# The opening loads of a two-layer encoder trunk, put into one fixed order on SyncE's queue

## The chip, the cores and the metric

The kernel runs on one core of a Trainium2 chip (trn2). Its time is the device time of one execution in microseconds (us). The engines are TensorE (PE, with its weight loads as PEld), VectorE (DVE), ScalarE (ACT), GpSimd (POOL) and SyncE (SP, which here only issues DMAs). The trace was taken by the hardware profiler in one execution; its times count from the start of that execution's span.

## The reference, cut to what matters

The trunk has two layers over x of 512 tokens by 1024 channels, all in float32, and a memory of 256 tokens by 1024. Only the start of the first layer matters here:

```python
for l in range(DEPTH):                       # DEPTH = 2
    h = rms_norm(x, norm_g[l])               # a sum of squares over 1024 channels per token
    proj = h @ w_in[l]                       # 7752 columns: three branches, gates, indexer
    ...
    mkv = rms_norm(mem, mem_norm_g[l]) @ w_mem_kv[l]
    mk, mv = jnp.split(mkv, 2, axis=-1)      # memory keys and values, 512 columns each
    y_mem = memory_attention(mq, mk, mv) * jax.nn.silu(mz)
    ...
    x = x + merged @ w_out[l]
return rms_norm(x, final_g)
```

## The kernel before

Every float32 product is made of three matmuls on parts in the type float32r: a value is split into hi (a cast on ACT) and lo (value minus hi, on DVE or POOL), and hi times hi, hi times lo and lo times hi are added up in PSUM. So each weight tile of 128x1024 (512 KB) that comes in through the tile `wraw` costs one cast to `whi` and one subtraction to `wlo`; each of these three names has four buffers.

The opening of the first layer needs four sets of loads, 7168 KB in all: `mem`, the memory (4 loads of 256 KB, line 257 in `load_mem`); the keys' weights `w_mk0` (512 KB for each of four steps, the first as two halves, lines 326 and 328); `x` (8 loads of 256 KB, line 339); and the values' weights `w_mv` (4 of 512 KB, line 166 in `raw_chunk`, called at line 345). All are issued by SyncE on one DMA queue. Each `w_mv` load takes a `wraw` buffer that a `w_mk0` tile held, so it has to wait until that tile's last subtraction (line 335) is done.

What is done with them, in PE's order, which the source fixes with `issue_after` (through `behind_pe`) from line 357 on:

- Lines 349 to 356: the key products, 96 matmuls of 256 columns, over `mem` and `w_mk0`. They are not scaled by the memory's norm yet; that is done later.
- Line 358, `norm_cols(sums)`: the sums of squares of x over its channels, 8 matmuls against a column of ones (each shows as two in the trace, on the tile `tr`). Before them ACT squares each x tile (line 228) and DVE adds the squares of tiles 1 to 6 to those of tile 0 (line 231); those of tile 7 go to PE by themselves. After them DVE (line 214) and POOL (line 215, a power) make the column 1/rms.
- Lines 368 to 370, `mem_v` of chunk 0: 12 matmuls of 512 columns. It needs chunk 0 of `w_mv` split (lines 346 and 347: casts behind the last square on ACT, subtractions on DVE).
- Line 372, `spread`: the norm of x is spread to a bank of PSUM, which `norm_x` (line 381, on DVE and ACT) needs to make h.
- `mem_v` of chunk 1; then the sums of squares of the memory (lines 376 to 380), which ACT squares (line 365) and POOL adds (line 367, behind the power of line 215); `mem_v` of chunk 2; `spread` of the memory's norm; `mem_v` of chunk 3.
- Line 437: the first projection of h, for the indexer; from there on PE works through the rest of the layer.

The framework's scheduler sets the order of the instructions on each engine, out of what is ready, by priorities from its own model. `issue_after(a)` adds an edge: the instructions traced in the block that run on the engine of `a` come behind `a` on it. It sets an order of issue, and no wait for `a` to end. Before the change no such edge bears on the loads: the `issue_after` at line 344 names an ACT instruction, and the load in its block is issued by SyncE.

Of the kernel before, what the change touches and what calls it, by code (L numbers as in the profile page):

```python
# [1 line left out]

# [1 line left out]

# [14 lines left out]
P = 128  # L19
# [4 lines left out]
KT = D // P  # L24
# [28 lines left out]
def kernel(  # L53
# [18 lines left out]
    nc = tc.nc  # L72
# [10 lines left out]
    on_pe, on_pool, on_act, on_dve, on_sp = [], [], [], [], []  # L83
# [8 lines left out]
    def nm(base):  # L92
        count[0] += 1
        return f"{base}_{count[0]}"
# [7 lines left out]
    def s2(base, dt=F32, shape=(P, S)):  # L102
        return work.tile(list(shape), dt, tag="s2", name=nm(base), bufs=N_S2)
# [60 lines left out]
    def raw_chunk(src, n=1024):  # L164
        raw = wpool.tile([P, 1024], F32, tag="wraw", name=nm("wraw"), bufs=4)
        nc.sync.dma_start(raw[:, :n], src)
        return raw
# [57 lines left out]
    def norm_add(sums, k, xk, n=S, apart=KT - 1):  # L225

        sq = s2("sq")[:, :n]
        on_act[:] = [A.activation(sq, xk, AF.Square)]
        last = on_act[0]
        if k not in (0, apart):  # L230
            last = V.tensor_add(sums[0], sums[0], sq)  # L231
        else:
            sums.append(sq)
        return last
# [18 lines left out]
    def load_mem(ks=range(0, KT, 2)):  # L253
        ms = []
        for k in ks:
            t = s2("mem", shape=(P, 2, M))
            on_sp[:] = [nc.sync.dma_start(t, memT[k * P:(k + 2) * P, :].rearrange("(a p) m -> p a m", p=P))]
            ms.append(t)
        return ms

    def mem_parts(l, m, k):
        hi = s2("memh", F32R, (P, 2, M))
        lo = s2("meml", F32R, (P, 2, M))
        for a in range(2):
            g = 20 * l + G_MEM + k + a
            on_dve[:] = [split_scaled(hi[:, a, :], lo[:, a, :], m[:, a, :], gains[:, g:g + 1])]
        return [hi[:, 0, :], hi[:, 1, :]], [lo[:, 0, :], lo[:, 1, :]]
# [50 lines left out]
    mem0, mh, ml, parts_k = [], [], [], []  # L318
    for i in range(4):
        raw, hi, lo = (wpool.tile([P, 1024], t, tag=g, name=nm(g), bufs=4)  # L320
                       for t, g in ((F32, "wraw"), (F32R, "whi"), (F32R, "wlo")))
        mem0 += load_mem((2 * i,))
        for a in range(2):
            if i == 0:
                c = slice(a * 512, (a + 1) * 512)
                nc.sync.dma_start(raw[:, c], w_mk0[i, :, c])
            elif a == 0:
                nc.sync.dma_start(raw, w_mk0[i])
        a, b = mem_parts(0, mem0[i], 2 * i)
        mh += a  # L330
        ml += b
        for a in range(2):
            c = slice(a * 512, (a + 1) * 512)
            A.copy(hi[:, c], raw[:, c])
            last = V.tensor_sub(lo[:, c], raw[:, c], hi[:, c])
        parts_k.append((hi, lo))
    x = [s2("x") for _ in range(KT)]
    for k in range(KT):
        nc.sync.dma_start(x[k], xT[k * P:(k + 1) * P, :])
    sums, parts_v = [], []  # L340
    for k in range(KT):
        last = norm_add(sums, k, x[k])
        if k in (1, 3, 5, 6):
            with tc.issue_after(on_act[0].ins):
                parts_v.append(raw_chunk(w_mv[0, len(parts_v)]))
    with tc.issue_after(on_act[0].ins), tc.issue_after(last.ins):
        parts_v[:2] = [split_chunk(raw, eng=V) for raw in parts_v[:2]]
    banks, pv = [pj(), pj()], [pj(), bank("pv")]
    for k in range(KT):
        hi, lo = parts_k[k // 2]  # L350
        for h in range(4):
            o = banks[h // 2][:, h % 2 * M:h % 2 * M + M]
            c = slice(k % 2 * 512 + h * P, k % 2 * 512 + h * P + P)
# [80 lines left out]
    for l in range(DEPTH):  # L434
# [420 lines left out]
        x = []  # L855
# [136 lines left out]
```

## Time and profile before

| | |
|---|---|
| median of 3 runs | 1077.87 us (1077.76 to 1078.63) |
| the profiled execution | 1077.09 us, of which the span of the trace is 1075.3 us |
| PE busy | 1054.9 us, 98% of the span |
| PE without work in the opening | 6.3 us, before the sums of squares of x |
| DMA in the opening | 7168 KB by about 23 us, close to 390 GB/s from 4 to 20 us |

The profiled execution's 1.8 us outside the span are what lies ahead of the first and behind the last instruction of the trace. In views of a stretch the busy time of PE is that of matmuls, which overlap each other; PEclk is the granted clock of TensorE, where 1.00 is 2.4 GHz and 0.50 is 1.2 GHz. On the rows of a timeline the text in brackets is the engine's idle time before that row, and what ended it. Rows that are marked SPq are the issues of DMAs by SyncE, not the transfers.

### The profile page before, as it was taken

Reading aid. Unit: us, or ns where it says so; the run is one execution under the profiler, and the core shown is the slowest. Engines: PE = TensorE matmul, PEld = TensorE weight load, DVE = VectorE, ACT = ScalarE, POOL = GpSimd, SP = SyncE. Lnnn points to the kernel's source line nnn. Section 1 sums busy time; section 2 is a strip of 40 time slices with the busy share of each in tenths; the row PEclk is TensorE's granted clock in tenths of the full one; section 3 lists DMA queues with packets and bytes.
Section 4 is the critical chain, followed back from the end, with each engine's and each line's share of the span. In section 5 each row is a group of like instructions: output and inputs, shape, how many; then the busy total and the mean of one; then the engine's idle time right before and its main releaser. Section 6 shows DMA issues by size and latency. Waiting matters only on the chain.

```text
span 1075.3 us, 13884 instructions
## 1 busy us (share of the span) xinstructions
PE 1054.9 (98%) x5108; PEld 889.5 (83%) x5108; DVE 704.1 (65%) x1305; ACT 477.3 (44%) x858; POOL 215.0 (20%) x296
## 2 busy tenths in 40 slices
PE   7999999999999999999999999999999999999997
PEld 6888888888788887888888888888888888788886
DVE  5857968787678855534465688787858887444343
ACT  6645454322465543433345555532235654333332
POOL 1400420000324411121250133100005323002101
PEclk8999999999999999999999999999999999999998
DMA  7454212323322222425444222121333222133312
GB/s 278 129 169 145 88 60 79 98 79 118 108 89 98 98 65 80 134 94 196 147 125 151 79 89 79 59 98 60 118 112 115 89 98 79 59 98 98 128 69 79
DMA packets 38804, 113.82 MB, mean 106 GB/s; under 512 B 4264, under 2 KB 8360, under 8 KB 38736
## 3 DMA queue, kind: packets, MB, share of 16 engines
q1 hardware_dynamic: 37440, 110.81, 31.0%
q10 hardware_dynamic: 1296, 2.12, 0.5%
q8 instruction: 40, 0.66, 0.2%
q14 instruction: 28, 0.23, 0.1%
HBM read 108.70 MB, written 6.84 MB: 107 GB/s over the span
## 4 chain that ended last, share of the span: by engine, by line
PE 92%; DVE 3%; ACT 1%; DMA 1%; issue 1%; POOL 1%; SPq 0%; POOLq 0%; DVEq 0%; ACTq 0%
PE pj L86 75%; PE at L86 7%; PE pv L86 5%; PE tr L547 2%; PE tr L86 2%; DVE wlo L151 1%; POOL sg L689 1%; DMA wraw<-in_w_mk 1%; DVE sq L231 1%; ACT whi L172 1%; DMA x<-in_xT 1%; DVE p L745 0%; DVE sg L685 0%; DVE stk L462 0%; ACT mgh L158 0%
## 5 line engine op out<-in xcount | busy, mean ns | idle before, releaser
L172 ACT CAST whi<-wraw 128x1024 fp32r<-128x1024 f32 (+1 forms) x174 | 181.7, 1046 | 369.7 <-PE pj L86 237.7
L86 PE MATMUL pj<-hh,whi 128*128 128x512 f32 (+1 forms) x848 | 330.1, 389 | 0.0
L86 PE MATMUL pj<-hl,whi 128*128 128x512 f32 (+1 forms) x848 | 328.8, 388 | 0.0
L86 PE MATMUL pj<-hh,wlo 128*128 128x512 f32 (+1 forms) x848 | 328.5, 387 | 0.0
L151 DVE TENSOR_TENSOR wlo<-wraw,whi 128x1024 fp32r<-128x1024 f32 x156 | 194.5, 1250 | 136.9 <-ACT whi L172 136.3
L86 PEld LDWEIGHTS pj<-hh,wlo 128*128 128x128 f32 x848 | 159.2, 188 | 32.1
L86 PEld LDWEIGHTS pj<-hh,whi 128*128 128x128 f32 x848 | 159.3, 188 | 31.0
L86 PEld LDWEIGHTS pj<-hl,whi 128*128 128x128 f32 x848 | 159.3, 188 | 30.7
L689 POOL TENSOR_TENSOR sg<-sg,sg 128x512 f32<-128x512 f32 x32 | 48.5, 1515 | 230.9 <-DVE sg L685 230.9
L86 PE MATMUL pj<-yh,whi 128*128 128x512 f32 x192 | 75.1, 391 | 0.0
L86 PE MATMUL pj<-yl,whi 128*128 128x512 f32 x192 | 74.8, 390 | 0.0
L86 PE MATMUL pj<-yh,wlo 128*128 128x512 f32 x192 | 74.8, 389 | 0.0
L731 POOL TENSOR_TENSOR p<-rel,acc 128x256 f32<-128x256 f32 (+2 forms) x48 | 60.1, 1276 | 0.0
L685 DVE SCALAR_TENSOR_TENSOR sg<-sg,pj 128x512 f32<-128x512 f32 x48 | 32.8, 685 | 36.7 <-PE pj L86 36.6
L86 PE MATMUL pj<-mgl,whi 128*128 128x512 f32 (+1 forms) x152 | 54.3, 357 | 0.3 <-DVE mgl L159 0.3
L86 PE MATMUL pj<-mgh,whi 128*128 128x512 f32 (+1 forms) x152 | 54.2, 357 | 0.0
L86 PE MATMUL pj<-mgh,wlo 128*128 128x512 f32 (+1 forms) x152 | 54.1, 356 | 0.0
L529 DVE MATCH_REPLACE8 acc<-m,acc 128x256 f32<-128x256 f32 (+2 forms) x96 | 51.4, 542 | 0.0
L745 DVE CUSTOM_DVE_ANT_0 p<-at,p 128x128 f32<-128x128 f32 (+1 forms) x64 | 29.4, 489 | 32.6 <-PE at L86 32.4
L528 DVE MAX8 m<-acc 128x8 f32<-128x256 f32 (+2 forms) x96 | 48.7, 547 | 0.0
L86 PEld LDWEIGHTS pj<-yh,wlo 128*128 128x128 f32 x192 | 36.0, 188 | 7.5
L86 PEld LDWEIGHTS pj<-yl,whi 128*128 128x128 f32 x192 | 36.1, 188 | 7.3
(211 smaller groups left out, 1683.3 us busy)
## 6 DMA issues: line engine op xcount, KB each, us to landing
wraw<-in_w_tiled SPq DMA_DIRECT2D x112, 512.0 KB, 3.4
wraw<-in_w_br SPq DMA_DIRECT2D x24, 512.0 KB, 3.5
wraw<-in_w_out SPq DMA_DIRECT2D x16, 512.0 KB, 3.4
wraw<-in_w_mv SPq DMA_DIRECT2D x8, 512.0 KB, 3.5
x<-in_xT SPq DMA_DIRECT2D x16, 256.0 KB, 5.4
wraw<-in_w_av SPq DMA_DIRECT2D x8, 512.0 KB, 3.9
rel<-bias_row SPq DMA_DIRECT2D x16, 256.0 KB, 3.9
wraw<-in_w_mk SPq DMA_DIRECT2D x7, 512.0 KB, 3.6
```

Source lines behind the costliest of these rows:

```text
L86: on_pe[:] = [T.matmul(*a, **kw)]
L151: eng.tensor_sub(out_lo, src, hi)
L172: A.copy(hi[:, :n], raw[:, :n])
L231: last = V.tensor_add(sums[0], sums[0], sq)
L528: V.max(m8, a[:, :n])
L529: V.match_replace(out=a[:, :n], in_to_replace=m8, in_values=a[:, :n], imm_value=TAKEN)
L547: T.transpose(pt[:, i * P:(i + 1) * P], col_of(qb, kb), ident)
L685: last = V.scalar_tensor_tensor(s, s, 1.0, ps, op0=ALU.add, op1=ALU.mult)
L689: G.tensor_add(acc[j], acc[j], s)
L731: G.tensor_add(p[:, Q_COL[qb]:Q_COL[qb] + n], rel[:, 512 - n:512], mb[:, :n])
L745: V.tensor_tensor_reduce(out=pq, in0=ps[:, :n], in1=pq, op0=ALU.add, op1=ALU.min, scale=-1.0, scalar=3e38, accum_out=st[:, 0, qb:qb + 1])
```

## The change

Each load of the opening is put behind the one before it by `issue_after` on SyncE: memory and keys' weights in turn, as they are written, then x tiles 0 to 5; behind x tile 5 both the first chunk of `w_mv` and x tile 6, which have no order between them; then x tile 7; and the `w_mv` chunks 1 to 3 behind x tile 7 (none of them is put behind chunk 0 or behind each other). The list `on_sp` holds the load that was issued last; `load_mem` already set it. No load, tile or buffer is added or taken away, and nothing changes in what ACT, DVE, POOL and PE compute.

```diff
+        with tc.issue_after(on_sp[0].ins) if on_sp else nullcontext():
+            mem0 += load_mem((2 * i,))
-        mem0 += load_mem((2 * i,))
         for a in range(2):
             if i == 0:
                 c = slice(a * 512, (a + 1) * 512)
-                nc.sync.dma_start(raw[:, c], w_mk0[i, :, c])
+                with tc.issue_after(on_sp[0].ins):
+                    on_sp[:] = [nc.sync.dma_start(raw[:, c], w_mk0[i, :, c])]
             elif a == 0:
-                nc.sync.dma_start(raw, w_mk0[i])
+                with tc.issue_after(on_sp[0].ins):
+                    on_sp[:] = [nc.sync.dma_start(raw, w_mk0[i])]
...
     x = [s2("x") for _ in range(KT)]
-    for k in range(KT):
-        nc.sync.dma_start(x[k], xT[k * P:(k + 1) * P, :])
     sums, parts_v = [], []
     for k in range(KT):
+        with tc.issue_after(on_sp[0].ins):
+            on_sp[:] = [nc.sync.dma_start(x[k], xT[k * P:(k + 1) * P, :])]
+        if k == 5:
+            with tc.issue_after(on_sp[0].ins):
+                parts_v.append(raw_chunk(w_mv[0, 0]))
+    with tc.issue_after(on_sp[0].ins):
+        parts_v += [raw_chunk(w_mv[0, c]) for c in range(1, 4)]
+    for k in range(KT):
         last = norm_add(sums, k, x[k])
-        if k in (1, 3, 5, 6):
-            with tc.issue_after(on_act[0].ins):
-                parts_v.append(raw_chunk(w_mv[0, len(parts_v)]))
     with tc.issue_after(on_act[0].ins), tc.issue_after(last.ins):
         parts_v[:2] = [split_chunk(raw, eng=V) for raw in parts_v[:2]]
```

## Rows read from the trace of the kernel before

**Rows 1.** The head of the profile's page: the span, the busy time of each engine with its share of the span and its instructions, and PE's busy tenths in 40 equal slices of the span.
```profile
span 1075.3 us, 13884 instructions
...
PE 1054.9 (98%) x5108; PEld 889.5 (83%) x5108; DVE 704.1 (65%) x1305; ACT 477.3 (44%) x858; POOL 215.0 (20%) x296
...
PE   7999999999999999999999999999999999999997
```

**Rows 2.** The waits of PE over the whole span: what it waited for, us in total, how often, the longest.
```profile
PE tr L86 <- DVE sq L231: 7.3, 2, 6.3
```

**Rows 3.** The chain of work that ended last, in order of time, where it passes through the opening: start, us, what.
```profile
19.47 0.64 ACT sq L228
...
24.11 0.70 DVE sq L231
...
24.95 3.55 PE tr L86 x16
```

**Rows 4.** SyncE's issues, in order of time: start, us from the first start to the last end, line, what is loaded, how many in the row.
```profile
3.18 0.97 SPq L328 DMA_DIRECT2D wraw<-in_w_mk  x2
4.19 0.44 SPq L257 DMA_DIRECT2D mem<-in_memT  x1
6.74 2.64 SPq L166 DMA_DIRECT2D wraw<-in_w_mv  x2
9.43 0.43 SPq L257 DMA_DIRECT2D mem<-in_memT  x1
11.05 1.64 SPq L166 DMA_DIRECT2D wraw<-in_w_mv  x2
12.75 5.25 SPq L339 DMA_DIRECT2D x<-in_xT  x8
```

**Rows 5.** The waits of SyncE's queue up to 19 us: line, what it waited for, us in total, how often, the longest.
```profile
SPq L166 <- DVE wlo L335: 5.2, 4, 1.9
SPq L403 <- DMA x<-in_xT: 0.8, 1, 0.8
```

**Rows 6.** DMA issues by size with the us from issue to landing, each for the one issue in a stretch: the first `w_mv` load (issued at 6.74) and the third (11.05).
```profile
wraw<-in_w_mv SPq DMA_DIRECT2D x1, 512.0 KB, 5.6
wraw<-in_w_mv SPq DMA_DIRECT2D x1, 512.0 KB, 4.9
```

**Rows 7.** ACT in order of time, from 9 to 30 us: start, us, line, operation, out<-in, how many.
```profile
10.39 1.15 ACT L334 CAST whi<-wraw 128x512 fp32r<-128x512 f32 x2 [0.18 <-DMA wraw<-in_w_mk]
...
14.73 0.91 ACT L158 ACTIVATE memh<-mem,gains 128x256 fp32r<-128x256 f32 x2 [2.39 <-DMA mem<-in_memT]
18.80 3.34 ACT L228 ACTIVATE sq<-x 128x512 f32<-128x512 f32 x5 [3.15 <-DMA x<-in_xT]
22.33 1.94 ACT L228 ACTIVATE sq<-x 128x512 f32<-128x512 f32 x3 [0.20 <-DMA x<-in_xT]
24.18 3.87 ACT L172 CAST whi<-wraw 128x1024 fp32r<-128x1024 f32 x4
27.95 2.19 ACT L365 ACTIVATE sq<-mem 128x512 f32<-128x512 f32 x4
```

**Rows 8.** DVE in order of time, from 20 to 31 us.
```profile
20.14 4.67 DVE L231 TENSOR_TENSOR sq<-sq,sq 128x512 f32<-128x512 f32 x6 [3.98 <-ACT sq L228]
25.24 2.36 DVE L176 TENSOR_TENSOR wlo<-wraw,whi 128x1024 fp32r<-128x1024 f32 x2 [0.43 <-ACT whi L172]
28.54 0.16 DVE L214 TENSOR_SCALAR rs_v<-tr 128x4 f32<-128x4 f32 x1 [0.94 <-PE tr L86]
```

**Rows 9.** POOL in order of time, from 28 to 35 us.
```profile
28.79 1.94 POOL L215 TENSOR_TENSOR rs_r<-rs_v,mhalf 128x4 f32<-128x4 f32 x1 [25.11 <-DVE rs_v L214]
30.70 4.15 POOL L367 TENSOR_TENSOR sq<-sq,sq 128x512 f32<-128x512 f32 x3
```

**Rows 10.** PE in order of time, single rows: the sums of squares of x, the first matmul of `mem_v` chunk 0 and the eighth, the sums of squares of the memory and the matmul behind them, and the first matmul of the indexer's projection.
```profile
24.95 3.55 PE L86 MATMUL tr<-ones,sq 128*128 128x1 f32 x16 [6.25 <-DVE sq L231]
28.36 0.77 PE L86 MATMUL pj<-whi,memh 128*128 128x512 f32 x1
...
31.49 0.42 PE L86 MATMUL pv<-wlo,memh 128*128 128x512 f32 x1
...
36.33 0.95 PE L86 MATMUL tr<-ones,sq 128*128 128x1 f32 x8
37.14 0.49 PE L86 MATMUL pj<-whi,memh 128*128 128x512 f32 x1
...
43.20 0.40 PE L86 MATMUL tr<-hh,whi 128*72 128x512 f32 x1
```

**Rows 11.** Stretches of the opening: us, then busy time of PE, PEld, DVE, ACT and POOL with their instructions, the granted clock, the DMA engines' share, GB/s.
```profile
20.00:22.00 2.00, 0.00 (x0) 0.00 (x0) 1.66 (x3) 1.85 (x4) 0.00 (x0) 0.82 0.93 322
...
30.00:32.00 2.00, 2.00 (x7) 1.51 (x7) 0.98 (x1) 0.14 (x1) 2.00 (x2) 0.62 0.87 244
```

**Rows 12.** The same view between the layers, where PE waits 1.08 us for the sum of squares of the second layer's x and has sums of squares until 545.7.
```profile
544.00:545.00 1.00, 0.20 (x2) 0.23 (x3) 0.65 (x1) 0.61 (x1) 0.10 (x1) 1.00 0.00 0
...
547.00:548.00 1.00, 1.00 (x7) 1.00 (x6) 0.00 (x0) 0.00 (x0) 1.00 (x2) 0.50 0.05 16
...
550.00:551.00 1.00, 1.00 (x10) 1.00 (x9) 0.00 (x0) 0.98 (x1) 0.00 (x0) 0.82 0.45 88
```

More of the change, by code (lines that the diff above doesn't have):

```diff
@@ L1 @@
-from contextlib import ExitStack
+from contextlib import ExitStack, nullcontext
 import numpy as np
```

## The prediction, made before the changed kernel was run

> **What bounds the kernel now.** Read the page's head first: matmuls fill 98% of the span, and PE's row of slices has a digit under 9 only in its first and last slice [rows 1]. So a microsecond counts only if it is taken off PE's path, and there is little to take. The view of waits then says where PE stands idle at all: 7.3 us in two waits for the squares of x, of which one is 6.3 us long [rows 2]. The chain of work shows that this wait is on the path that sets the end: a square on ACT, the additions on DVE up to 24.11 + 0.70 = 24.81, and 0.14 us later PE's sums of squares at 24.95 [rows 3]. Then ask what the squares wait for. ACT stood idle 3.15 us until x tile 0 was there at 18.80, and again until tile 5 came at 22.33 [rows 7]; ACT takes 3.34 / 5 = 0.67 us a tile, and DVE six additions in 4.67 us, started at 20.14 [rows 8]. The arrival of x sets all of it. And x is late because its first issue is at 12.75, behind all four `w_mv` loads, which in turn waited 5.2 us for `wraw` buffers [rows 4, 5].
>
> A second cost sits behind the wait. The granted clock falls to half in the stretch 20 to 22 (mean 0.82, so 0.36 of 2 us lost: from about 21.3) and is back in the stretch 30 to 32 (mean 0.62, back at about 31.5) [rows 11]. The 16 small matmuls of the sums take 28.36 - 24.95 = 3.41 us there; 8 of the same kind take 37.14 - 36.33 = 0.81 us at the full clock, so 16 would take 1.62: 1.8 us lost [rows 10]. Seven matmuls of `mem_v` take 31.49 - 28.36 = 3.13 us; at the full clock 24 of them and a short spread fill 37.14 to 43.20, so they start about 0.23 us apart and seven take 1.6: 1.5 us lost [rows 10]. Together 3.3 us. From 24.95 to the first projection of h at 43.20 PE has 18.25 us with no wait, 14.95 of them work at the full clock [rows 10].
>
> **The change, part by part.** It issues the same loads in another order. No instruction of a compute engine is added, and no byte.
>
> The arrival table. In the trace the queue lands loads in the order of issue, so the KB that were issued up to a load give its landing. By order [rows 4]: 2560 KB with the last key weights, landed 10.39 [rows 7]; 3328 with `w_mv` 0, 6.74 + 5.6 = 12.34 [rows 4, 6]; 4096 with the last `mem`, 14.73 [rows 7]; 4608 with `w_mv` 2, 11.05 + 4.9 = 15.95 [rows 4, 6]; 5376 with x tile 0, 18.80; 6656 with x tile 5, 22.33, thus 0.71 us for each 256 KB [rows 7]. I read the new order off this table. Memory and keys are 3072 KB, x tiles 0 to 5 reach 4608 KB: tile 5 lands at about 15.95. If `w_mv` 0 goes next, it lands at 5120 KB, about 17.9, x tile 6 at 18.8, x tile 7 at 5632 KB, 19.5. Then `w_mv` 1, 2 and 3 at 20.9, 22.3 and 23.7.
>
> Sums of squares of x: tile 7 at 19.5, ACT 0.65, so 20.15; DVE's last addition (of tile 6) starts at 18.8 + 0.65 and ends by 20.2; with the 0.14 us of before PE starts at 20.3. That is 24.95 - 20.3 = **4.65 us** earlier. DVE no longer runs behind: additions of 0.70 keep pace with tiles 0.71 apart.
>
> Key products: `mem` tiles 1 to 3 come earlier and key weights 1 to 3 at 256 to 512 KB more of queue, that is 0.7 to 1.3 us later (the last one at about 11.7 and not 10.39). PE ended them at 24.95 - 6.25 = 18.70, with waits of some 1 us in them; I expect 17.5 to 18.7. It costs nothing either way, since PE then waits until 20.3; if that cover went, every us after 20.3 would cost one.
>
> Chunk 0 of `w_mv`, now later: landed 17.9, cast behind the last square (20.15 + 1.05 = 21.2; four casts take 3.87 [rows 7]), subtraction 1.2 (two take 2.36 [rows 8]), ready at 22.4. PE ends the sums at 20.3 + 1.62 = 21.9 at the full clock, at 23.7 at half. So it costs 0 to 0.5 us; I take 0, the row with the clock at half.
>
> Chunks 2 and 3 and the memory's squares: chunk 3 lands at 23.7, cast to 24.75; if ACT squares the memory behind its casts as now, two squares are done at 25.85 (four in 2.19 [rows 7]); POOL's three additions of 4.15 [rows 9] end at 30.0; from PE's sums of these squares (36.33) to the first projection (43.20) are 6.87 us [rows 10]. So the projection can't start before 36.9 in that order: the gain is capped at 43.20 - 36.9 = **6.3 us**.
>
> SyncE's own queue: the in-flight limit that the trace shows is a wait of 0.8 us of the load of line 403 that ended when x tile 0 landed, eight loads earlier [rows 5, 7]. With it the ninth load (key weights 3) waits for the first, which is in by then, and the loads in flight are still at least 2 MB, so the queue doesn't run dry. `w_mv` 1 to 3 need `wraw` buffers that the key splits free at 9 to 14; they issue later than that. The loads behind them on SyncE (line 403 on, then the projection's weights, which wait for the splits of `w_mv` anyway) move forward with PE.
>
> The clock: whether it falls can't be read off the old rows directly, so bounds. No better than before: 0. Not falling at all: 3.3 us back. The nearest row is between the layers: there PE waited only 1.08 us and had short sums until 545.7, and the clock was at half from 547 until about 550.6 [rows 12]. A wait of 20.3 - 18 = 2 us or more with 16 such sums behind it is the stronger case, so I expect a fall, with a shorter stretch at half. I take 0.55 us back of the 3.3.
>
> The Trainium skill ("TensorE: Matmul & The Clock Gate", section "Why this matters for your kernels") tells authors to avoid long idle gaps of PE between bursts, since they bring the lower clock; by it the shorter wait might cost no clock, and the sum would be the cap, 6.3 us. The fall after 1.08 us [rows 12] speaks against that.
>
> Sum: 4.65 + 0.55 = 5.2 us. After 43.2 PE has no wait that depends on anything but its own progress, so the shift lasts to the end. Against the profiled execution: span 1075.3 - 5.2 = 1070.1, plus 1.8 us outside it, 1071.9. The median of the runs is 0.8 above that execution, so I forecast **1072.7**.
>
> **The rivals.**
> - **x goes wholly ahead.** Nothing orders `w_mv` 0 against x tile 6, so the scheduler may put tiles 6 and 7 first. Tile 7 then lands at 5120 KB, 17.85, and the sums start at 18.65, 6.3 us earlier; chunk 0 lands at 19.5, is split by 21.8, while PE's sums last until 20.3 to 22.1. The gain meets the cap: 6.2 us, **1071.6**. For it: the square of tile 6 comes before the cast of chunk 0. Against: chunk 0 is traced first and is a longer load.
> - **The clock stays up.** Same arrivals, 4.65 + 3.3, less 0.5 for chunk 0, held by the cap to 6.3: **1071.6**. Against it stand rows 12.
> - **Order of issue is not order of landing.** If the loads that are in flight together (eight or so) share the queue, moving x up by 2 MB of issues moves its landing little, and the norm waits as before: **1077.9**. The landings of the table are in order of issue, which speaks against it. The Trainium skill ("DMA: Bandwidth & Descriptors", section "Queues, rings and completion order") says that completion is not first in, first out for an issuing engine; by it this is possible, but no landing here is out of order.
> - **Slower: the clock stays down through all of `mem_v`.** With the values' weights last, PE gets its work in pieces: a wait before the sums, for chunk 0, for the power of POOL (1.94 us [rows 9]), for the memory's squares. If these keep the clock at half until the projection, the 14.95 us of work take 29.9: 20.3 + 29.9 = 50.2, 7.0 us later than 43.20, **1084.9**. It decides from the point where the loss exceeds 4.65 + 3.3 = 7.95 us, so from 15.9 us of PE time at half on. Against it: once PE had dense matmuls at 28.36, the clock was up after 3.1 us [rows 10, 11].
>
> **How the numbers follow.** Forecast 0.57; x wholly ahead 0.20; clock up 0.06; order not kept, or the gain eaten by an equal wait, 0.11; slower 0.06. A shift also changes whether the clock falls between the layers, where 3.6 us at half cost 1.8 [rows 12]: ±1.8 for all cases. So the forecast's own range is 1071 to 1075; with the cap, the lost dip and half of the shift at the other end the range is 1070.2 to 1076.0, which leaves out the last two cases. About 0.2%, 2.2 us, is what a measurement here can tell from no change. Faster by more: 0.82; within: 0.12; slower: 0.06.
>
> **What would show it.** SyncE's x issues start near 5 us and ACT's first square of x near 12.5; PE's wait before the sums falls from 6.25 to 2 to 3 us and ends at about 20.3; the granted clock has a shorter stretch at half; the first projection starts at 38.0 ± 1, and the rest of the trace is the old one, moved. A start of the sums near 18.6 shows the first rival; sums near 24 the third; new waits of PE between 24 and 37 that hold the clock at half the last. It would be wrong if the scheduler, given other edges, orders later work differently and makes a wait there, which no row of before can show.

## The result, and the profile after

| | before | changed |
|---|---|---|
| median | 1077.94 us (1077.76 to 1078.63, 4 runs) | 1071.79 us (1070.82 to 1073.45, 4 runs) |
| ratio | | 0.9943, 95% interval 0.9926 to 0.9961 |
| the profiled execution, span in brackets | 1077.09 (1075.3) | 1073.45 (1071.7) |

The changed kernel is 6.1 us faster by the medians, where 5.2 were forecast. A second series of the same kernel (the first experiment) gives 5.3. The profiled execution is the longest of the first series, and its span is only 3.6 us shorter. So two things have to be explained: why that trace falls 1.6 us short of the sum, and why other executions do better than it. In what follows line numbers from the opening on are up to 6 higher than before, and in some of the experiments' kernels up to 10.

The page's head answers to [rows 1]: PE has the same work, in a shorter span.

```profile
span 1071.7 us, 13880 instructions
...
PE 1054.6 (98%) x5108; PEld 889.8 (83%) x5108; DVE 705.7 (66%) x1305; ACT 477.4 (45%) x858; POOL 214.4 (20%) x296
```

The waits of PE over the span answer to [rows 2]: 2.3 us of the 7.3 are gone, all of them from the wait in the opening (6.3, now 3.9).

```profile
PE tr L86 <- DVE sq L231: 5.0, 2, 3.9
```

PE in order of time, single rows, as in [rows 10]: the sums of x, the sums of the memory, the first projection of h, and between the layers the sums of the second layer's x.

```profile
21.95 3.44 PE L86 MATMUL tr<-ones,sq 128*128 128x1 f32 x16 [3.90 <-DVE sq L231]
...
33.43 0.95 PE L86 MATMUL tr<-ones,sq 128*128 128x1 f32 x8
...
40.30 0.40 PE L86 MATMUL tr<-hh,whi 128*72 128x512 f32 x1
...
541.86 1.02 PE L86 MATMUL tr<-ones,sq 128*128 128x1 f32 x8 [1.08 <-DVE sq L231]
```

The sums start 24.95 - 21.95 = 3.00 us earlier, and the projection 43.20 - 40.30 = 2.90. Between the two lie 18.35 us, against 18.25: in this execution the shorter wait gave no clock back. From the projection to the end of the span it is 1071.7 - 40.30 = 1031.4, against 1032.1. Thus 3.0 - 0.1 + 0.7 = 3.6.

What held the sums at 21.95, and not at the forecast's 20.3, is seen in the chain of work, which now passes through the loads (start, us, what):

```profile
5.87 7.02 DMA wraw<-in_w_mk
...
12.90 7.52 DMA x<-in_xT
...
20.45 0.64 ACT sq L228
...
21.11 0.70 DVE sq L231
...
21.95 3.44 PE tr L86 x16
```

x tile 6 is issued at 12.90, at the moment when the last key weights land (5.87 + 7.02 = 12.89), and needs 7.52 us. SyncE's issues, as in [rows 4], show that the key weights are the eighth load before it, and two loads in the queue that the forecast had not put there:

```profile
2.19 0.43 SPq L409 DMA_DIRECT2D oh<-in_onehot  x1
...
3.64 0.43 SPq L410 DMA_DIRECT2D rb<-in_rel_bias  x1
...
5.87 0.38 SPq L331 DMA_DIRECT2D wraw<-in_w_mk  x1
6.29 4.91 SPq L344 DMA_DIRECT2D x<-in_xT  x6
11.67 0.33 SPq L166 DMA_DIRECT2D wraw<-in_w_mv  x1
12.90 1.01 SPq L344 DMA_DIRECT2D x<-in_xT  x2
14.30 1.68 SPq L166 DMA_DIRECT2D wraw<-in_w_mv  x3
```

`oh` (80 KB, line 403 before) and `rb` (1 KB, line 404) belong to the bias of the attention. Before the change they stood at 18.79 and 19.47, behind all of the opening's loads. No edge of the change names them, and the scheduler now issues them as the fourth and the seventh load. ACT answers to [rows 7]: the first x tile is there at 13.96, 4.84 us earlier than before, but ACT then waits 1.56 us for tile 5 and 1.32 for tile 6.

```profile
13.96 2.97 ACT L228 ACTIVATE sq<-x 128x512 f32<-128x512 f32 x5
18.49 0.63 ACT L228 ACTIVATE sq<-x 128x512 f32<-128x512 f32 x1 [1.56 <-DMA x<-in_xT]
20.45 1.30 ACT L228 ACTIVATE sq<-x 128x512 f32<-128x512 f32 x2 [1.32 <-DMA x<-in_xT]
```

Windows of 2 us as in [rows 11] (the last three columns are the granted clock, the DMA engines' share and GB/s). From 6 to 10 us the queue moves 316 and 344 GB/s, where before it moved 398 in each of the two. The clock is at half from about 22 to 28.9, and falls again between the layers:

```profile
6.00:8.00 2.00, 2.00 (x19) 2.00 (x19) 1.41 (x4) 1.40 (x3) 0.00 (x0) 1.00 0.91 316
8.00:10.00 2.00, 2.00 (x19) 2.00 (x18) 1.48 (x3) 1.53 (x3) 0.00 (x0) 1.00 0.96 344
...
22.00:24.00 2.00, 2.00 (x11) 2.00 (x11) 1.29 (x2) 1.90 (x3) 0.00 (x0) 0.52 0.15 59
...
28.00:30.00 2.00, 2.00 (x10) 1.63 (x8) 0.00 (x0) 0.02 (x1) 1.92 (x2) 0.78 0.94 250
...
544.00:546.00 2.00, 2.00 (x13) 2.00 (x12) 0.00 (x0) 0.00 (x0) 2.00 (x2) 0.58 0.04 14
```

### The profile page after: what moved, and what is told of

Read it like the earlier page. It is cut to its first block, busy times and chain, and to the rows that moved or that the text cites. A ratio compares the mean times of both kernels' runs of the same rounds, so it can differ in the third digit from the quotient of the medians.

```text
span 1071.7 us, 13880 instructions
## 1 busy us (share of the span) xinstructions
PE 1054.6 (98%) x5108; PEld 889.8 (83%) x5108; DVE 705.7 (66%) x1305; ACT 477.4 (45%) x858; POOL 214.4 (20%) x296
## 4 chain that ended last, share of the span: by engine, by line
PE 93%; DVE 2%; DMA 2%; ACT 1%; issue 1%; POOL 1%; SPq 0%; POOLq 0%; ACTq 0%; DVEq 0%
PE pj L86 76%; PE at L86 8%; PE pv L86 5%; PE tr L553 2%; PE tr L86 2%; DMA wraw<-in_w_mk 1%; DMA x<-in_xT 1%; DVE wlo L151 1%; POOL sg L695 1%; ACT whi L172 1%; DVE sq L231 0%; DVE sg L691 0%; ACT mgh L158 0%; DVE o L919 0%; DVE p L751 0%
```

## The experiments

The theory: the whole gain is the earlier arrival of x, it is cut by the two bias loads at the front, and what is left of the wait costs the clock. Rivals: the fixed order of memory and keys gives part of the gain; the loads share the queue, and `w_mv` 0 ahead of tile 6 is the loss; the clock has nothing to do with the wait. All diffs are against the changed kernel unless another is named, and all ratios are to the kernel before.

**The same kernel again** (`after_again`).

> The changed kernel once more, as the ground for the others of this group. If the spread of its runs (1070.8 to 1073.5 us so far) is the granted clock's, the runs with the higher mean clock are the fast ones, the order of instructions being the same: 1070.8 to 1073.5 again, with some 2 us between clock 0.995 and 0.993. If it is the arrival of x that varies, the time doesn't go with the clock.

Median 1072.42 us (1070.9 to 1074.25, 5 runs), ratio 0.9948 [0.9935, 0.9962]. In its trace the sums start at 21.65 and the projection at 39.78:

```profile
21.65 3.54 PE L86 MATMUL tr<-ones,sq 128*128 128x1 f32 x16 [3.91 <-DVE sq L231]
```

The runs spread by 3.35 us, and in this series the spread goes with the mean granted clock of the execution: 0.995 at 1070.9, 0.992 at 1074.25; 1071 x (0.995 / 0.992 - 1) = 3.2 us. Other series don't show this. In that of `bias_loads_late` 1071.56 us has 0.993 and 1071.79 has 0.995, and in that of `before_filled` the seven runs at 0.995 lie between 1074.48 and 1078.38. So the clock is not the whole of the spread.

**Memory and keys left to the scheduler; only x and `w_mv` ordered** (`x_order_only`).

```diff
-        with tc.issue_after(on_sp[0].ins) if on_sp else nullcontext():
-            mem0 += load_mem((2 * i,))
+        mem0 += load_mem((2 * i,))
...
-                with tc.issue_after(on_sp[0].ins):
-                    on_sp[:] = [nc.sync.dma_start(raw, w_mk0[i])]
+                on_sp[:] = [nc.sync.dma_start(raw, w_mk0[i])]
```

> The part of the change that puts x ahead of the values' weights, without the edges on memory and keys' weights, which the scheduler orders as before. Theory 1 (all of the gain is x moving ahead of 1.5 to 2 MB of weights): the sums start within 1 us of the changed kernel's 21.65 to 21.95, the time is 1071.5 to 1073. Theory 2 (the order of memory and keys has a share, since the last memory tile came behind two chunks of values' weights): the key products end later, the time is 1074 to 1076.

1073.23 us (1072.3 to 1074.22, 4 runs), 0.9956 [0.9942, 0.9969]. PE's sums of x:

```profile
21.86 3.54 PE L86 MATMUL tr<-ones,sq 128*128 128x1 f32 x16 [2.13 <-DVE sq L231]
```

They start within 0.1 us of the changed kernel's. `oh` and `rb` are early here too (4.83 and 5.57), so they don't come from the edges on memory and keys.

**Memory and keys ordered, x behind all of `w_mv`** (`keys_order_only`).

```diff
+    for c in range(4):
+        with tc.issue_after(on_sp[0].ins):
+            parts_v.append(raw_chunk(w_mv[0, c]))
+        on_sp[:] = on_ld
     for k in range(KT):
         with tc.issue_after(on_sp[0].ins):
             on_sp[:] = [nc.sync.dma_start(x[k], xT[k * P:(k + 1) * P, :])]
-        if k == 5:
-            with tc.issue_after(on_sp[0].ins):
-                parts_v.append(raw_chunk(w_mv[0, 0]))
-    with tc.issue_after(on_sp[0].ins):
-        parts_v += [raw_chunk(w_mv[0, c]) for c in range(1, 4)]
```

> The other part: memory and keys' weights in the changed order, then the values' weights, then x, as x was before. Theory 1: x tile 7 comes no earlier, the sums start at 24.9 to 26 (the two small bias loads go to the front here too), the key products end about 1 us sooner for nothing, the time is 1077.7 to 1079. Theory 2 (memory and keys have a share of the gain): 1074 to 1076.

(`on_ld` holds the load that `raw_chunk` issued.) 1079.22 us (1078.22 to 1080.08, 10 runs), 1.0011 [1.0002, 1.0020]: nothing gained, a little lost. The sums, after a wait longer than that of before:

```profile
26.55 3.54 PE L86 MATMUL tr<-ones,sq 128*128 128x1 f32 x16 [7.63 <-DVE sq L231]
```

With the run before this settles the first rival: x's place in the queue is the gain.

**x wholly ahead of the values' weights** (`x_wholly_first`).

```diff
-        if k == 5:
-            with tc.issue_after(on_sp[0].ins):
-                parts_v.append(raw_chunk(w_mv[0, 0]))
     with tc.issue_after(on_sp[0].ins):
-        parts_v += [raw_chunk(w_mv[0, c]) for c in range(1, 4)]
+        parts_v += [raw_chunk(w_mv[0, c]) for c in range(4)]
```

> All four chunks of the values' weights behind x tile 7. Theory 1 (the arrival of x tile 7 sets the start of PE's sums): 512 KB less ahead of tiles 6 and 7 bring them 1.3 us sooner, the sums start at 20.6 us and not 21.95, and the time is 1 us under the changed kernel's, 1070.8. Theory 2 (the weights' chunk 0 takes its place): it lands at 21.1, is split by 23.4, PE waits for it behind the sums, and the time is the changed kernel's, 1071.8.

1070.98 us (1070.82 to 1073.72, 5 runs), 0.9939 [0.9926, 0.9952]. The sums start at 20.06, the projection at 37.50, so 5.7 us earlier than before:

```profile
20.06 2.10 PE L86 MATMUL tr<-ones,sq 128*128 128x1 f32 x16 [1.83 <-DVE sq L231]
```

Against the two traces of the changed kernel the sums are 1.6 to 1.9 us earlier, so `w_mv` 0 ahead of tile 6 does cost arrival. The interval overlaps the changed kernel's; that it is better is not shown by the times.

**The two bias loads behind x** (`bias_loads_late`).

```diff
-        nc.sync.dma_start(oh, onehot)
-        nc.sync.dma_start(rb, rel_bias)
+        with tc.issue_after(on_sp[0].ins):
+            nc.sync.dma_start(oh, onehot)
+            nc.sync.dma_start(rb, rel_bias)
```

> The changed kernel with the two small loads for the bias (80 KB and 1 KB on 32 partitions, which went to the front of the queue) put behind x tile 7. Theory 1 (these two slow the queue between 4 and 10 us): key weights and x land about 1 us sooner, the sums start at 20.9, the time is 1070.8. Theory 2 (the lag of x tiles 5 to 7 comes from the queue itself with eight loads in flight): the sums start at 21.7 to 21.95, the time is within 0.3 us of the changed kernel's.

1071.66 us (1071.23 to 1071.79, 5 runs), 0.9938 [0.9924, 0.9952]. The chain, then windows, then PE's row:

```profile
4.70 7.12 DMA wraw<-in_w_mk
...
11.84 7.02 DMA x<-in_xT
...
18.88 0.64 ACT sq L228
```

```profile
6.00:8.00 2.00, 2.00 (x18) 1.93 (x18) 1.67 (x4) 1.40 (x4) 0.00 (x0) 1.00 1.00 375
8.00:10.00 2.00, 2.00 (x19) 2.00 (x18) 1.55 (x3) 1.93 (x5) 0.00 (x0) 1.00 1.05 402
```

```profile
20.39 2.83 PE L86 MATMUL tr<-ones,sq 128*128 128x1 f32 x16 [2.63 <-DVE sq L231]
```

Without the two loads the forecast's numbers appear in this trace: tile 6 at 18.88 (18.8), the sums at 20.39 (20.3), the projection at 38.71 (38.0 ± 1). The times don't show a gain: the interval overlaps the changed kernel's.

Tile 6 lands 1.56 us earlier here, and 81 KB account for only 0.2 of that at 398 GB/s. By the windows up to 10 us the queue moved 228 KB less in the changed kernel (16, 292, 335, 316 and 344 GB/s against 9, 274, 357, 375 and 402, each for 2 us), that is 0.6 us more. The traces also record the landing of each load in sixteen parts; ACT started on tile 6 in the changed kernel at 20.45, behind the last of them. The eighth part of tile 6 landed at 17.93 in the changed kernel and at 17.45 here, the fifteenth at 18.69 and 17.81, the last at 20.42 and 18.86. So only 0.5 us of the delay is in the middle of the load, and some two thirds of it are in its last parts.

In both traces the last part falls behind the fifteenth from one load to the next: behind tile 4 in the changed kernel, where the last parts of tiles 4 and 5 are at 16.27 and 18.47 (the fifteenth at 16.08 and 16.75), and behind tile 5 here. Just then a load of instructions (16 KB on a queue of its own) starts, at 16.13 and at 15.03 us. It takes 14.0% and 13.4% of 16 engines in 0.5 us, which is 1.1 us of one DMA engine. The row of the changed kernel from 16.0 to 16.5, then that of `bias_loads_late` from 15.0 to 15.5:

```profile
q8 instruction: 1, 0.02, 14.0%
```

```profile
q8 instruction: 1, 0.02, 13.4%
```

All fourteen traces have such a load, starting between 14.2 and 17.5 us. That it is what holds the last part up fits in time; no experiment moved it.

**One of the two early, one late** (`small_one_early`: `rb`, 1 KB, at the front; `onehot_early`: `oh`, 80 KB, at the front; one execution each). The diff is that of the first against `bias_loads_late`; the second has it the other way round.

```diff
         with tc.issue_after(on_sp[0].ins):
             nc.sync.dma_start(oh, onehot)
-            nc.sync.dma_start(rb, rel_bias)
+        nc.sync.dma_start(rb, rel_bias)
```

> The changed kernel with only the 80 KB bias load behind x tile 7; the 1 KB one stays near the front. If the bytes or the 32 partitions of the 80 KB load slow the queue, x tile 6 lands near 18.9 us as with both late, and the sums start near 20.4. If it is the slot that any load takes among the eight in flight, it lies halfway or near the changed kernel's, 19.6 to 20.4 and 21.1 to 21.9.

> The changed kernel with only the 1 KB bias load behind x tile 7; the 80 KB one stays at the front. If the 80 KB load is the cause, x tile 6 lands at 19.9 to 20.4 us and the sums start at 21.4 to 21.95, as in the changed kernel; if the small one is, 18.9 and 20.4.

1069.55 and 1069.54 us. ACT's last two squares of each, `small_one_early` first:

```profile
18.98 1.31 ACT L228 ACTIVATE sq<-x 128x512 f32<-128x512 f32 x2 [1.92 <-DMA x<-in_xT]
```

```profile
19.20 1.31 ACT L228 ACTIVATE sq<-x 128x512 f32<-128x512 f32 x2 [2.56 <-DMA x<-in_xT]
```

With one of the loads in front tile 6 is at most about 0.3 us later than with none. With `w_mv` 0 ahead of it, it was there at 20.45, 20.15, 20.36 and 19.53 in four traces with both loads in front, and at 18.88 and 19.01 in two with none: 0.5 to 1.6 us later.

The records of landing split this too (`x_order_only`, the 20.36, left out, since its memory and keys have another order). The eighth part of tile 6 landed at 17.45 and 17.38 with none in front, at 17.58 and 17.64 with one, and at 17.93, 17.81 and 17.75 with both. So the two loads add up to 0.3 to 0.5 us there. The last part came 1.4 to 1.6 us behind the eighth with none or one, and 2.5, 2.3 and 1.8 with both. This lag is the larger share of the delay in two of the three traces, and it differs by 0.7 us among the three, which have the same loads in the same order. Why it was longer with both loads in front is not settled.

**PE's wait filled** (`after_filled`: 11 matmuls on a tile of the kernel ahead of the sums, whose result nobody reads).

```diff
+    with behind_pe():
+        ps = bank("at")
+        for i in range(11):
+            matmul(ps[:, :P], busy, busy, start=True, stop=True)
     with behind_pe():
         r = norm_cols(sums)
```

> The changed kernel with 11 matmuls of 128 columns on a tile of ones, whose result nobody reads, between the key products and the sums of squares of x: they fill PE's wait from 17.9 to 21.95 (0.34 us each, 3.75 us). Theory 1 (the clock falls because of this wait, and costs 3.3 us behind it): the clock stays at 2.4 GHz, the sums take 1.6 us and not 3.4, from the start of the sums to the first projection 15 to 16 us pass and not 18.35, and the time is 2.5 us under the changed kernel's, 1069.3. Theory 2 (the split of the weights' chunk 0 and the memory's squares are late next): PE waits there instead and the time is within 1 us of the changed kernel's.

1071.34 us (1070.14 to 1072.78, 5 runs), 0.9937 [0.9924, 0.9949]. PE's sums of the memory and first projection, and the window that is at 0.52 in the changed kernel:

```profile
30.54 1.05 PE L86 MATMUL tr<-ones,sq 128*128 128x1 f32 x8 [0.31 <-POOL sq L377]
...
37.47 0.40 PE L86 MATMUL tr<-hh,whi 128*72 128x512 f32 x1
```

```profile
22.00:24.00 2.00, 2.00 (x14) 1.83 (x15) 2.00 (x2) 1.90 (x3) 0.00 (x0) 1.00 0.07 29
```

The clock stays at 1.00 through the whole opening and the projection starts at 37.47, 2.83 us ahead of the changed kernel's, with the sums 0.80 earlier: about 2 us of this are clock. Yet the median is only 1.1 us under that of `after_again`, which was measured beside it. The mean clock of its five runs goes from 0.994 to 0.997 and the profiled one has 0.997, so the others lost clock in places that no trace shows. Of the forecast price of the clock, 3.3 us, this trace shows 2, and the medians 1.1, with intervals that overlap.

**The same fill in the kernel before** (`before_filled`: 26 such matmuls, against the kernel before).

> The kernel before with 26 matmuls of 128 columns on a tile of ones, whose result nobody reads, in PE's wait from 18.7 to 24.95. It prices the clock alone, with x as late as before. Theory 1 (the fall behind the wait costs 3.3 us): no stretch at half in the opening, 14.95 us from the sums to the first projection and not 18.25, the time 1074.6. Theory 2 (part of it is taken back by the power on POOL and the memory's squares, as when the changed kernel was filled): the time 1076 to 1077.

1075.88 us (1074.08 to 1078.38, 10 runs), 0.9982 [0.9972, 0.9992]: 2.1 us gained, less than the 3.3 that [rows 10] give for the clock. In its trace x came late (tile 0 at 20.28, with fifteen of its sixteen parts there at 18.59), the fill ran out, and after a wait of 1.82 us the clock fell all the same, for 3.4 us in place of 10.2:

```profile
28.00:30.00 2.00, 2.00 (x9) 1.67 (x9) 2.00 (x3) 2.00 (x4) 0.86 (x1) 0.63 0.48 142
```

**Both: x wholly first and the bias loads late** (`x_first_bias_late`), the two diffs above together.

> Both mended: all values' weights behind x tile 7, and the two bias loads behind it as well. Theory 1 (landing follows the KB issued ahead): x tile 6 lands at 16.9 and 7 at 17.9, the sums start at 18.7, right behind the key products; then chunk 0 (landed 19.5, split by 21.8) and the memory's squares are late next, the first projection starts near 36.9 and the time is 1070.3. Theory 2 (nothing is left to gain behind x wholly first): 1070.9 to 1071.2.

1073.51 us (1071.51 to 1073.91, 5 runs), 0.9955 [0.9942, 0.9967]: sums at 19.57, the earliest so far, and no gain over the changed kernel. PE's sums of x and of the memory, POOL's additions, DVE's subtractions, and a window:

```profile
19.57 1.92 PE L86 MATMUL tr<-ones,sq 128*128 128x1 f32 x16 [0.50 <-DVE sq L231]
...
29.96 1.05 PE L86 MATMUL tr<-ones,sq 128*128 128x1 f32 x8 [1.37 <-POOL sq L370]
```

```profile
23.48 6.42 POOL L370 TENSOR_TENSOR sq<-sq,sq 128x512 f32<-128x512 f32 x3
```

```profile
24.57 4.21 DVE L176 TENSOR_TENSOR wlo<-wraw,whi 128x1024 fp32r<-128x1024 f32 x2 [0.25 <-ACT whi L172]
```

```profile
32.00:34.00 2.00, 2.00 (x6) 1.54 (x6) 2.00 (x4) 0.84 (x2) 1.07 (x1) 0.50 0.77 217
```

This is the mechanism of the forecast's cap: PE now waits for the memory's squares, and the clock falls behind that wait instead. The projection starts at 38.48. POOL's three additions take 6.42 us, and DVE's two subtractions beside them 4.21; before they took 4.15 and 2.36 [rows 8, 9].

**The cap moved** (`x_first_mem_apart`: the kernel just above, but POOL adds only three of the four squares and PE sums the fourth by itself).

```diff
-            if k > 0:
+            if k in (1, 2):
                 G.tensor_add(sq[0], sq[0], sq[-1])
...
-        for a in range(2):
-            square_sums(col, sq[0][:, a, :], 2, a == 0, a == 1)
+        for i, (t, a) in enumerate((t, a) for t in (sq[0], sq[3]) for a in range(2)):
+            square_sums(col, t[:, a, :], 2, i == 0, i == 3)
```

> The kernel with both mended (values' weights and bias loads behind x), whose PE waited 1.37 us for POOL's three additions of the memory's squares (6.4 us) and then lost the clock: here POOL makes two of these additions, and the last square goes to PE by itself, 8 more short matmuls (0.8 us). Theory 1 (the memory's squares on POOL are what is late next): the wait is gone, the clock stays up, the first projection starts at 36.2 and not 38.5, the time is 1070 to 1070.5, under x wholly first. Theory 2 (PE now waits for the power and the splits of the values' weights instead, and the clock falls all the same): 1072 to 1073.5.

1072.78 us (1070.05 to 1074.85, 6 runs), 0.9951 [0.9937, 0.9964]. The wait for POOL is gone, and the projection comes at 37.63. But in this trace the clock fell at about 22, behind a wait of 1.45 us, and the gain over the changed kernel is again not to be told from none.

**Bias loads late and the wait filled** (`bias_late_filled`), the diffs of `bias_loads_late` and `after_filled` together.

> Both edits at once: the two bias loads behind x tile 7, and 11 idle matmuls on a tile of the kernel, whose result nobody reads, in PE's wait before the sums. If the two are what the forecast missed (the arrival of x and the clock), x tile 6 is there near 18.9, the sums start at 20.4 to 20.6 with the clock full from there on, and the first projection is held by the memory's squares at about 36.9 to 37.2, so 3.1 to 3.4 us ahead of the changed kernel's 40.3: 1069.0 to 1070.5, ahead of both kernels. The rival: what the sums gain is given back in full at the memory's squares or in the dip of the clock between the layers, and the time is that of either edit alone, 1071 to 1072.5.

1070.87 us (1069.03 to 1071.58, 5 runs), 0.9934 [0.9921, 0.9948]: the lowest median of the kernels that were run more than once. PE's sums of x and of the memory, and first projection:

```profile
21.12 1.84 PE L86 MATMUL tr<-ones,sq 128*128 128x1 f32 x16
...
30.14 1.05 PE L86 MATMUL tr<-ones,sq 128*128 128x1 f32 x8 [0.48 <-POOL sq L377]
...
37.10 0.40 PE L86 MATMUL tr<-hh,whi 128*72 128x512 f32 x1
```

The profiled execution is what the first theory expected (1069.46 us, the clock at 1.00 throughout the opening, the projection held by POOL's additions at 37.1), except that the fill was some 0.6 us too long and moved the sums to 21.12; behind the cap that cost nothing. The median is 0.4 us above the expected range: three of the five runs lie above it, all with a mean clock of 0.995, where the other two have 0.997. Its interval overlaps that of either edit alone and the changed kernel's.

## Why the prediction was right, step by step

- **What bounds the kernel.** Right. The gain is PE's wait for the squares of x; `x_order_only` has 4.7 us of it, with an interval that overlaps the changed kernel's, `keys_order_only` none. From the projection on the trace is the old one, moved: 1032.1 and 1031.4 us to the end.
- **The arrival table.** Right where only the named loads are ahead, 18.88 and 20.39 in `bias_loads_late` for 18.8 and 20.3, and 19.01 for 18.8 in `bias_late_filled`. The table takes landings of one trace as fixed by KB alone; the lag of a load's last part, which the traces show to vary, is no term of it.
- **The step that failed** is the sentence on SyncE: "The loads behind them on SyncE (line 403 on, …) move forward with PE". They moved forward by 16 us, to the front of the queue. The term of 4.65 us measured 3.00 in the profiled execution and 3.30 in the second trace; with the two loads late it measured 24.95 - 20.39 = 4.56. That the two loads delay the middle of tile 6 by 0.3 to 0.5 us is shown; that they cause the rest, the lag of its last part, is not. The forecast named reordering as what would make it wrong, and looked for it in later work on PE only.
- **What else was costed at nothing** was nothing. The key products ended at 21.95 - 3.90 = 18.05 (17.5 to 18.7 forecast), PE had no wait between the sums and `mem_v` of chunk 0, and none at the sums of the memory. The wait for the load eight places earlier is there as forecast, and is a link of the chain.
- **The clock.** 0.55 us were taken as regained, between bounds of 0 and 3.3; the two traces of the changed kernel give -0.1 and 18.25 - (39.78 - 21.65) = 0.1. The windows say why. Time at half in a window of 2 us is 4 x (1 - granted clock). Before, it adds up to 10.2 us, from about 21.3 to 31.5, and the first 3.6 of them lay in PE's wait and cost nothing: 6.6 us of work at half. Now it is 6.8 us from about 22.1 on, all of it work. The stretch is shorter, as forecast, but all of what went had lain in PE's wait. The wait would have had to be shorter still: over the traces the clock was at half for 10.2 us behind waits of 6.25 and 7.63 us at the sums, for 6.8 behind 2.13 to 3.91 (four traces), for 3.4 behind 1.45 to 1.83 (five traces), and not at all behind 0.50 or a wait filled to its end.
- **The total.** The medians lie lower than the two traces, which are the longest run of the first series and the second longest of the next. So most other executions did better than the traced ones, and no trace shows how. More clock is one candidate: the fastest runs of the two series have a mean clock of 0.995, the slowest 0.993 and 0.992. An earlier landing of x is another: with the same loads in the same order tile 6 was there at 20.45, 20.15 and 19.53. So why the total came out at 5.3 to 6.1 us with a first term of 3.0 to 3.3 stays open. The forecast of 1072.7 owes part of its accuracy to luck: its first term was 1.4 to 1.7 us too large, and what came on top of that term was some 2 to 3 us and not 0.55.
- **Between the layers.** PE waits 1.1 us there in every trace. In six of the fourteen traces (before included) the clock fell behind that wait; these need 1031.4 to 1033.4 us from the projection to the end, the other eight 1030.4 to 1031.6. The means differ by 1.5 us, near the ±1.8 that the range allowed for. The forecast read 3.6 us at half off [rows 12]; they give 3.4, since the window from 550 to 551 at 0.82 holds 0.36 us of it, and so 1.7 us of time and not 1.8.
- **The cap of 6.3 us** (projection not before 36.9). No trace is under it, and two come near: 37.10 in `bias_late_filled` and 37.47 in `after_filled`, both held by POOL's additions for the memory. The Trainium skill's advice against idle gaps ("TensorE: Matmul & The Clock Gate", section "Why this matters for your kernels") holds here as far as the two fills show it, with the clock full in both openings.
- **The rivals.** Order of landing held. "x goes wholly ahead" didn't happen by itself (`w_mv` 0 was issued first), and as an experiment gave 1070.98, where 1071.6 was worked out. The slow case, the clock down through all of `mem_v`, happened nowhere: the longest stretch at half behind the sums of the changed kernel was 6.8 us, against the 15.9 that it needed.

## What to carry to other kernels

An order that is written out for some instructions of a queue moves the others too: list everything that the scheduler may put on that queue, and give the loads that are not urgent an edge of their own. When a wait is shortened, find the next thing that is late before sizing the gain, here POOL's additions of the memory's squares. Where the clock falls in some executions and not in others, take the size from several runs and the mechanism from the trace, and don't expect the two to agree to a microsecond.

## What the runs showed of the hardware

- **POOL and DVE slow each other when POOL adds and DVE subtracts.** POOL's additions of two SBUF tiles take 4.15 us for three when DVE has no such work beside them [rows 9], 6.42 when DVE subtracts at the same time, and DVE's subtractions 2.1 us each instead of 1.2. `x_wholly_first` shows the same pair (6.45 and 4.22). The Trainium skill ("SBUF — State Buffer", section "SBUF: two separate sides") says that a DVE operation with two SBUF inputs and a GpSimd operation that reads SBUF exclude each other on a shared pair of ports; the traces agree in that both lose. So x earlier brings work into collision that lay apart before. The power on POOL that makes 1/rms shows the opposite: 1.94 us before, with two subtractions on DVE beside it [rows 8, 9], and 1.03 in the three kernels with x wholly first, where DVE was idle for the first half of it.
- **In this program a load waits to be issued until the one eight places before it has landed.** x tile 6 at 12.90 for 12.89 in the changed kernel, 11.84 for 4.70 + 7.12 = 11.82 in `bias_loads_late`. In the traces SyncE's loads report their landing on eight semaphores, taken in turn, so the limit may be the program's; no run tells whether the chip has one.
- **The last of a load's sixteen parts can lag.** Of x tile 6 it came 0.4 to 3.0 us behind the eighth in the fourteen traces, 1.6 in that of the kernel before.
- **The queue is slower early in the opening with both bias loads among the first seven**: 326 to 349 GB/s from 6 to 10 us in five traces, against 362 to 392 in the four with neither in front. The cause stays open.
